# Block 1's first 32 tokens take their expert activations from gathered rows of u: the dense expert layer works on 352 columns

## The chip, the cores and the metric

The kernel runs on one core of a Trainium2 chip. The metric is the device time of one execution in microseconds, the median of several runs. The engines are TensorE (PE), VectorE (DVE), ScalarE (ACT), GpSimd (POOL) and SyncE (SP), which only issues DMAs; ACT and POOL issue DMAs too. Each works through its own queue in order.

## The reference, cut to what matters

One decoder layer on 512 tokens of width 1024, in float32: norm, two kinds of attention, output projection, norm, and then the expert layer below, a last norm. The change is in the expert layer alone. It has 16384 experts of one neuron each; every token chooses 16 of them in each of 8 heads.

```
def chunk(xc):
    q = (xc @ wq).reshape(PEER_CHUNK, PEER_HEADS, 2, PEER_HALF)
    s = jnp.einsum('chpd,hpkd->chpk', q, subkeys)
    s1, i1 = lax.top_k(s[:, :, 0], PEER_TOPK)
    s2, i2 = lax.top_k(s[:, :, 1], PEER_TOPK)
    ...
    eidx = jnp.take_along_axis(cidx, ci, axis=-1)
    g = jax.nn.softmax(cs, axis=-1)
    ug = jnp.take(u_table, eidx, axis=0)
    vg = jnp.take(v_table, eidx, axis=0)
    hid = jnp.einsum('cd,chkd->chk', xc, ug)
    a = jax.nn.gelu(hid, approximate=False) * g
    return jnp.einsum('chk,chkd->cd', a, vg)
```

## The kernel before, in words

Tokens lie in four blocks of 128. Block 0 gets its experts by index: for each of 128 choices a row of u, later a row of v, is gathered for all 128 tokens by an indirect DMA that POOL issues (`gathers`, L488); DVE multiplies a row of u with the tokens and sums (L505), and adds a row of v with its weight to `acc` (L512). The gathered rows go through `rowp`, a pool of four buffers.

Blocks 1 to 3 (384 tokens, `DT`) go through all 16384 experts densely. The experts are cut in 64 items of 256 (`NPAIR`), each of two halves of 128 (c). An item has a hidden part and an output part. Hidden: the item of u is loaded (`wraw`) and split into a high and a low half, whi by ACT (L123) and wlo by DVE (L124); for each half of the item `mm3` (L152) makes 24 matmuls of 128 x 384 into `pj`, and ACT takes the gelu (`hidden`, L526). Output: the gelu is multiplied by the token's gates (DVE, L783), split into ah (ACT) and al (DVE), and multiplied with the item of v, which is loaded and split into vh and vl in the same way: 36 matmuls of 128 x 512 into six accumulators `oa` (L806).

The gates of a token for all 16384 experts are a table, built in the spill stage: `pairs` (L604) chooses experts and gates for a block, `table` (L686) makes one-hot matrices o1, o2 and og (o1 times the gate, as two halves in f16) for eight tokens on DVE, PE multiplies them (L722), ACT copies the result into `gs` (L712), and SP writes it to `Gd` in DRAM, one write for 32 tokens (`GT`).

While that goes on, PE computes the hidden part of the first 28 items (`SPILL`) and writes their gelus to `Hd` in DRAM (`spill`, L535). The dense stage (`dense`, L768) then does the output part of all 64 items, and the hidden part of the other 36 between them; for the 28 it reads `Hd` back (ga). Stored and fresh items alternate by two. The gathers of block 0 run beside the dense stage.

The order: `merge` (L60) interleaves these streams by weights, and the framework then schedules each engine's instructions, and the buffers of the pools, by priorities; what it made is fixed for each engine. In the dense stage DVE's order is that of the code.

Of the kernel before, what the change touches and what calls it, by code (L numbers as in the profile page):

```python
# [10 lines left out]
F32 = mybir.dt.float32  # L11
# [20 lines left out]
NKEY = 128  # L32
DT = T - P
EPS = 1e-6
NEG = -1e30
# [5 lines left out]
NB = 8  # L41
GT = 32
NG = DT // GT
# [28 lines left out]
def tile_kernel(ctx: ExitStack, tc: tile.TileContext, x, w_in, w_f, b_f, w_out, wq, skT, u, v, uT, g1, g2, g2r, gfr,  # L72
# [9 lines left out]
    hres = gdram.tile([T, D], F32, name="hres")  # L82
    Hd = [gdram.tile([P, 2, DT], F32, name=f"Hd{n}") for n in range(SPILL)]

# [147 lines left out]
    with ExitStack() as st:  # L232
# [222 lines left out]
        for c in range(D // WC):  # L455
# [4 lines left out]
            for b in range(0, TB, 2):  # L460
# [62 lines left out]
    def hidden(uu, c, out_):  # L523
        ps = pj.tile([P, T], F32, name="pj")
        mm3(ps[:, :DT], [(uu[0][:, c, k, :], uu[1][:, c, k, :]) for k in range(KC)], XD)
        nc.scalar.activation(out_, ps[:, :DT], AF.Gelu)  # L526

    with ExitStack() as st:
        hsp = pool("hsp", bufs=HB, stack=st)
        rq = pool("rq", stack=st)  # L530
        vv = [rq.tile([P, 2 * NHEAD, TOPK], F32, name=f"vv{b}") for b in range(TB)]
        ii = [rq.tile([P, 2 * NHEAD, TOPK], U32, name=f"ii{b}") for b in range(TB)]
        rp = pool("rp", bufs=2, stack=st)

        def spill(fd, n0, n1):  # L535
            for n in range(n0, n1):
                uu = fd.get()
                hs = hsp.tile([P, 2, DT], F32, name="hs")
# [58 lines left out]
        with ExitStack() as s2:  # L597
# [6 lines left out]
            def pairs(b):  # L604
# [60 lines left out]
                if b == 0:  # L665
                    nc.vector.scalar_tensor_tensor(eidx, res[:, 0, :], float(NKEY), res[:, 1, :], op0=ALU.mult, op1=ALU.add)
                    return
                pt = ptr.tile([P, 3, P], F32, name="ptr")
                for n, src in enumerate((res[:, 0, :], res[:, 1, :], gg.rearrange("p h k -> p (h k)"))):
# [8 lines left out]
                nc.scalar.activation(tg2[:, 0], trg[:, :, None].to_broadcast([P, P, 2]), AF.Copy)  # L678
                nc.vector.tensor_tensor(tg2[:, 1], trg[:, :, None].to_broadcast([P, P, 2]), tg2[:, 0], ALU.subtract)
                yield 2.0  # L680
                for t0 in range(0, P, NB):
                    yield from table(b, t0, tri, tg2)

            tab, work = {}, []

            def table(b, t0, tri, tg2):  # L686
                ts_ = slice(t0, t0 + NB)
                pair = [P, NB, NKEY // 2, 2]

                def pairs_of(t):  # L690
# [3 lines left out]
                o2 = ohp.tile([P, NB, NKEY], F16, name="o2")  # L694
                nc.vector.tensor_tensor(pairs_of(o2), ib, tri[:, 1, ts_, None, :].to_broadcast(pair), ALU.is_equal)
                o1 = ohp.tile([P, NB, NKEY], F16, name="o1")
                nc.vector.tensor_tensor(pairs_of(o1), ib, tri[:, 0, ts_, None, :].to_broadcast(pair), ALU.is_equal)
                og = ohp.tile([P, 2, NB, NKEY], F16, name="og")
                for n in range(2):
                    nc.vector.tensor_tensor(pairs_of(og[:, n]), pairs_of(o1), tg2[:, n, ts_, None, :].to_broadcast(pair), ALU.mult)  # L700
                work.append([b, t0, o2, og, None])
                yield from advance()

            def advance():
                if len(work) > 2 or (work and work[0][4]):
                    b, t0, _, _, pgs = work.pop(0)
                    g = (b - 1) * (P // GT) + t0 // GT
                    if t0 % GT == 0:
                        tab[g] = gsp.tile([P, NKEY, GT], F32, name="gs")
                    for n, pg in enumerate(pgs):  # L710
                        q0 = t0 % GT + 4 * n
                        nc.scalar.activation(tab[g][:, :, q0:q0 + 4].rearrange("p i t -> p t i"), pg, AF.Copy, scale=1.0 / GS)  # L712
                    if t0 % GT == GT - NB:
                        nc.sync.dma_start(Gd[g], tab.pop(g).rearrange("p i t -> p (i t)"))
                for w in work[:-1] if len(work) > 1 else work:
                    if w[4] is None:
                        w[4] = []
                        for t4 in range(0, NB, 4):
                            pg = pgt.tile([P, 4, NKEY], F32, name="pg")
                            for tt in range(4):  # L720
                                for n in range(2):
                                    nc.tensor.matmul(pg[:, tt, :], w[2][:, t4 + tt, :], w[3][:, n, t4 + tt, :], start=(n == 0), stop=(n == 1))  # L722
                            w[4].append(pg)
                yield 2.8

            def gates3():
                for b in range(1, TB):
                    yield from pairs(b)
                while work:
                    yield from advance()  # L730

            L2 = 12.8 + 4.0 + 1.5 + 7.4
            merge((pairs(0), L2), (spill(feed, 0, D0_SPILL), 2.0 * D0_SPILL))
            ga = gathers()
            n1 = SPILL - D0_SPILL
            merge((gates3(), RF * 3 * (L2 + 1.0 + 2.8 * P // NB)), (spill(feed, D0_SPILL, SPILL), 2.0 * n1), (take(ga, D_GATHER), float(D_GATHER)))

    with ExitStack() as st:
# [9 lines left out]
        def load_v(i):  # L748
            if i < NPAIR:
# [3 lines left out]
                if i % 2 == 0:  # L753
# [4 lines left out]
                    gts[i + 1] = gt[:, :, 2:4, :]  # L758
                gas[i] = ep.tile([P, 2, DT], F32, name="ga")
                if n < SPILL:  # L760
# [159 lines left out]
```

## Time and profile before

Median of three runs: 1548.09 us (1547.84 to 1548.88). The profiled execution took 1545.79 us, of which the trace spans 1543.7.

| engine | busy us | share of the span |
|---|---|---|
| PE | 1503.6 | 97% |
| DVE | 1204.2 | 78% |
| ACT | 652.0 | 42% |
| POOL | 371.3 | 24% |

By time: attention and norms up to about 309 us, the query stage to about 403, the spill stage to 704, the dense stage to 1526, the last norm to the end. Busy time is a share over stages with different limits, so it has to be read stage by stage. Matmuls overlap, so what one costs is read from the distance between starts or from a run of them on the chain, not from its length; on DVE, too, an instruction's length overlaps the next by some 0.08 us.

### The profile page before, as it was taken

How to read it: one execution, taken by the hardware profiler on the slowest of the kernel's cores; microseconds unless marked ns; L12 is line 12 of the kernel's file. 1: busy time of each engine (PE TensorE's matmuls, PEld its weight loads, DVE VectorE, ACT ScalarE, POOL GpSimd, SP SyncE). 2: the span in 40 equal slices, each digit the busy share in tenths (PEclk: the TensorE clock that was granted, in tenths of full speed). 3: DMA queues.
4: the chain of work that ended last, by engine and by line, in shares of the span. 5: the costliest groups of instructions: out<-in, count | busy, mean ns of one | idle time of the engine just before them, and what ended most of it. 6: DMA issues, size and time to landing. Idle time of an engine off the chain costs nothing.

```text
span 1543.7 us, 22288 instructions
## 1 busy us (share of the span) xinstructions
PE 1503.6 (97%) x8689; PEld 1339.1 (87%) x8689; DVE 1204.2 (78%) x2250; ACT 652.0 (42%) x809; POOL 371.3 (24%) x273
## 2 busy tenths in 40 slices
PE   7999999999998999999999999999999999999997
PEld 6787888988898898998888899888989888989886
DVE  7555466559999999795788877778787888777886
ACT  6355454422234858485323333333333333333332
POOL 2000000000001000001344444444443443444441
PEclk9999999999999999999999999999999999999999
DMA  6211113322155757569999989999999999999984
GB/s 198 83 55 56 55 55 124 115 101 86 66 185 184 303 214 280 207 262 336 382 338 362 334 328 341 325 349 342 315 351 335 329 360 326 333 329 342 328 284 158
DMA packets 139353, 380.26 MB, mean 246 GB/s; under 512 B 9392, under 2 KB 58800, under 8 KB 134512
## 3 DMA queue, kind: packets, MB, share of 16 engines
q1 hardware_dynamic: 96400, 230.44, 42.1%
q0 software_dynamic: 37664, 134.96, 23.7%
q10 hardware_dynamic: 5184, 13.45, 2.4%
q8 instruction: 68, 1.11, 0.3%
q14 instruction: 37, 0.30, 0.1%
HBM read 338.90 MB, written 40.37 MB: 246 GB/s over the span
## 4 chain that ended last, share of the span: by engine, by line
PE 81%; DVE 12%; ACT 3%; DMA 2%; issue 1%; SPq 0%; ACTq 0%; DVEq 0%
PE pj L152 40%; PE oa L806 33%; DVE wlo L124 3%; PE o L427 2%; PE pg L722 2%; PE s L377 1%; PE t L404 1%; DVE og L700 1%; ACT gs L712 1%; PE xt L140 1%; ACT whi L123 1%; PE psc L587 1%; DMA gt<-Gd 1%; DMA Gd<-gs 1%; DVE eq L659 0%
## 5 line engine op out<-in xcount | busy, mean ns | idle before, releaser
L152 PE MATMUL pj<-xh,whi 128*128 128x384 f32 (+2 forms) x1304 | 454.8, 349 | 5.2 <-ACT hs L526 2.9
L152 PE MATMUL pj<-xh,wlo 128*128 128x384 f32 (+2 forms) x1304 | 453.0, 347 | 1.5 <-DVE wlo L124 1.5
L152 PE MATMUL pj<-xl,whi 128*128 128x384 f32 (+2 forms) x1304 | 452.0, 347 | 0.0
L496 POOL DMA_INDIRECT row<-in_u_dram,eidx x128 | 183.9, 1437 | 706.4 <-DVE hid L505 441.2
L123 ACT ACTIVATE whi<-wraw 128x2048 fp32r<-128x2048 f32 (+1 forms) x89 | 169.7, 1906 | 252.3 <-PE pj L152 244.3
L152 PEld LDWEIGHTS pj<-xh,whi 128*128 128x128 f32 x1304 | 245.8, 188 | 18.5 <-issue 4.7
L152 PEld LDWEIGHTS pj<-xh,wlo 128*128 128x128 f32 x1304 | 246.0, 189 | 11.9 <-DVE wlo L124 2.1
L152 PEld LDWEIGHTS pj<-xl,whi 128*128 128x128 f32 x1304 | 246.0, 189 | 10.2
L124 DVE TENSOR_TENSOR wlo<-wraw,whi 128x2048 fp32r<-128x2048 f32 (+1 forms) x89 | 202.5, 2275 | 61.9 <-ACT whi L123 61.9
L806 PE MATMUL oa<-vh,ah 128*128 128x512 f32 x768 | 238.5, 391 | 2.2 <-ACT ah L123 2.2
L806 PE MATMUL oa<-vh,al 128*128 128x512 f32 x768 | 238.1, 390 | 0.3 <-DVE al L124 0.3
L806 PE MATMUL oa<-vl,ah 128*128 128x512 f32 x768 | 238.0, 390 | 0.0
L496 POOL DMA_INDIRECT row<-in_v_dram,eidx x128 | 177.9, 1390 | 227.0 <-DVE acc L512 196.5
L123 ACT ACTIVATE vh<-vr 128x2048 fp32r<-128x2048 f32 x64 | 122.8, 1919 | 226.9 <-PE oa L806 175.8
L512 DVE SCALAR_TENSOR_TENSOR acc<-row,a,acc 128x1024 f32<-128x1024 f32 x128 | 164.2, 1283 | 23.4 <-DMA row<-in_v_dram,eidx 20.6
L505 DVE CUSTOM_DVE_ANT_0 row<-row,xn 128x1024 f32<-128x1024 f32 x128 | 152.5, 1221 | 29.8 <-DMA row<-in_u_dram,eidx 29.6
L806 PEld LDWEIGHTS oa<-vh,al 128*128 128x128 f32 x768 | 144.5, 188 | 31.4 <-DVE al L124 0.7
L806 PEld LDWEIGHTS oa<-vl,ah 128*128 128x128 f32 x768 | 144.4, 188 | 30.5
L806 PEld LDWEIGHTS oa<-vh,ah 128*128 128x128 f32 x768 | 144.0, 188 | 30.3 <-ACT ah L123 2.5
L124 DVE TENSOR_TENSOR vl<-vr,vh 128x2048 fp32r<-128x2048 f32 x64 | 146.3, 2285 | 0.0
L124 DVE TENSOR_TENSOR al<-ga,ah 128x768 fp32r<-128x768 f32 x64 | 61.3, 958 | 64.4 <-ACT ah L123 64.4
L712 ACT ACTIVATE gs<-pg 128x512 f32<-128x512 f32 x96 | 97.4, 1153 | 18.5 <-PE pg L722 18.1
(207 smaller groups left out, 1588.8 us busy)
## 6 DMA issues: line engine op xcount, KB each, us to landing
wraw<-in_uT_dram SPq DMA_DIRECT2D x64, 1024.0 KB, 6.5
vr<-in_v_dram SPq DMA_DIRECT2D x64, 1024.0 KB, 7.1
Gd<-gs SPq DMA_DIRECT2D x12, 2048.0 KB, 6.7
gt<-Gd SPq DMA_DIRECT2D x32, 768.0 KB, 9.3
wraw<-in_w_in_dram SPq DMA_DIRECT2D x12, 1024.0 KB, 4.8
Hd<-hs ACTq DMA_DIRECT2D x28, 384.0 KB, 3.6
ga<-Hd SPq DMA_DIRECT2D x28, 384.0 KB, 9.0
wraw<-in_wq_dram SPq DMA_DIRECT2D x8, 1024.0 KB, 4.8
```

Source lines behind the costliest of these rows:

```text
L123: nc.scalar.activation(hi, src, AF.Copy)
L124: nc.vector.tensor_sub(lo, src, hi.bitcast(F32))
L140: nc.tensor.matmul(pt[:, kc % 2, e, :], src[:, e, kc * P:(kc + 1) * P], diag[:, e, :], start=True, stop=True)
L152: nc.tensor.matmul(ps, a, c, start=(i == 0), stop=(i == 3 * n - 1))
L377: nc.tensor.matmul(s[:, :n], qs[:, part, h, i * P:n], kT[:, h, :n], start=(part == 0), stop=(part == 1 and g >= 2))
L427: nc.tensor.matmul(o[e * HD:(e + 1) * HD, pr, :], vs[:, j, h * HD:(h + 1) * HD], pts[e][:, j * P:(j + 1) * P], start=(j == 0), stop=(j == i))
L496: nc.gpsimd.indirect_dma_start(out=rows[n], out_offset=None, in_=tab, in_offset=bass.IndirectOffsetOnAxis(ap=eidx[:, k:k + 1], axis=0))
L505: nc.vector.tensor_tensor_reduce(out=t, in0=t, in1=xn0, scale=1.0, scalar=0.0, op0=ALU.mult, op1=ALU.add, accum_out=hid0[:, k:k + 1])
L512: nc.vector.scalar_tensor_tensor(acc, t, a0[:, k:k + 1], acc, op0=ALU.mult, op1=ALU.add)
L712: nc.scalar.activation(tab[g][:, :, q0:q0 + 4].rearrange("p i t -> p t i"), pg, AF.Copy, scale=1.0 / GS)
L722: nc.tensor.matmul(pg[:, tt, :], w[2][:, t4 + tt, :], w[3][:, n, t4 + tt, :], start=(n == 0), stop=(n == 1))
L806: nc.tensor.matmul(oacc[b][d], w[:, c, sl], m[:, c, d * 512:(d + 1) * 512], start=s0, stop=s1)
```

## The change

The first 32 tokens of block 1 leave the hidden part of the dense layer, which works on `DH` = 352 columns. Their activations come from u rows: 32 gathers, in each of which the 128 partitions hold 32 tokens times four groups of choices (`gatherq`), a dot product for each on DVE against `xnq`, the 32 tokens' normed x four times over (written to DRAM as `xqd` and read back), then gelu and gate. Their table therefore holds gate times gelu, in three bf16 parts instead of two f16 ones, and is built last (`tableq`). In the dense stage the other eleven groups are multiplied in place in `gt`, and `gt` is what is split. `SPILL` is 34 instead of 28, `HB` (buffers for hs) 3 instead of 4, and block 1's choice comes before the tables, merged with four items of its own.

```
-SPILL = 28
+SPILL = 34
 D0_SPILL = 4
+D1_SPILL = 4
-HB = 4
+HB = 3
...
-    XD = [(xh[:, k, P:], xl[:, k, P:]) for k in range(KC)]
+    XD = [(xh[:, k, P + GT:], xl[:, k, P + GT:]) for k in range(KC)]
...
+                        for d in range(2):
+                            sd = slice(d * 512, (d + 1) * 512)
+                            xq = hp.tile([GT, 512], F32, name="xq")
+                            nc.vector.scalar_tensor_tensor(xq, hb[0:GT, 1, sd], rs[0:GT, 1:2], g2b[0:GT, sd], op0=ALU.mult, op1=ALU.mult)
+                            nc.scalar.dma_start(xqd[:, sd], xq)
...
+        for s_ in range(NS):
+            nc.scalar.dma_start(xnq[s_ * GT:(s_ + 1) * GT, :], xqd)
...
+            def gatherq():
...
+                        nc.gpsimd.indirect_dma_start(out=rows[k], out_offset=None, in_=u,
+                                                     in_offset=bass.IndirectOffsetOnAxis(ap=eq4[:, k:k + 1], axis=0))
+                for k in range(3):
+                    issue(k)
+                for k in range(HK // NS):
+                    issue(k + 3)
+                    t = rows.pop(k)
+                    nc.vector.tensor_tensor_reduce(out=t, in0=t, in1=xnq, scale=1.0, scalar=0.0, op0=ALU.mult,
+                                                   op1=ALU.add, accum_out=hq4[:, k:k + 1])
+                    yield 1.0
+
+            def tableq():
+                nq = HK // NS
+                for s_ in range(NS):
+                    nc.vector.tensor_copy(aq[0:GT, s_ * nq:(s_ + 1) * nq], hq4[s_ * GT:(s_ + 1) * GT, :])
+                nc.scalar.activation(aq[0:GT], aq[0:GT], AF.Gelu)
+                nc.vector.tensor_mul(aq[0:GT], aq[0:GT], gq)
...
+                for t0 in range(0, GT, NB):
+                    yield from table(t0, t0, trq, tq3, BF16, 1.0)
...
-                for n in range(2):
-                    nc.vector.tensor_tensor(pairs_of(og[:, n]), pairs_of(o1), tg2[:, n, ts_, None, :].to_broadcast(pair), ALU.mult)
+                og = [og[:, 0], og[:, 1]] + ([lp.tile([P, NB, NKEY], dtype, name="og3")] if nparts > 2 else [])
+                for n in range(nparts):
+                    nc.vector.tensor_tensor(pairs_of(og[n]), pairs_of(o1), tg[:, n, ts_, None, :].to_broadcast(pair), ALU.mult)
...
             merge((pairs(0), L2), (spill(feed, 0, D0_SPILL), 2.0 * D0_SPILL))
+            n1 = D0_SPILL + D1_SPILL
+            merge((pairs(1), L2 + 2.0), (spill(feed, D0_SPILL, n1), 2.0 * D1_SPILL))
             ga = gathers()
-            n1 = SPILL - D0_SPILL
-            merge((gates3(), RF * 3 * (L2 + 1.0 + 2.8 * P // NB)), (spill(feed, D0_SPILL, SPILL), 2.0 * n1), (take(ga, D_GATHER), float(D_GATHER)))
+            merge((gates3(), RF * (2 * L2 + 7.0 + 3 * 2.8 * P // NB)), (spill(feed, n1, SPILL), 2.0 * (SPILL - n1)), (gatherq(), 1.2 * HK / NS),
+                  (take(ga, D_GATHER), float(D_GATHER)))
...
-                        a = ga_[:, c, :].rearrange("p (g t) -> p g t", t=GT)
-                        nc.vector.tensor_mul(a, gt[:, :, c, :], a)
+                        a = gt[:, 1:, c, :]
+                        nc.vector.tensor_mul(a, a, ga_[:, c, :].rearrange("p (g t) -> p g t", t=GT))
...
-                    split(ah, al, ga_)
+                    split(*[t.rearrange("p c (g t) -> p c g t", t=GT) for t in (ah, al)], gt.rearrange("p g c t -> p c g t"))
```

Three places show what this does to the order. POOL's queue, from its first gather on, in the kernel before (row_n is a buffer's use, eidx the indices of block 0):

```order
L496 DMA row_4557<-in_u_dram,eidx_99 128x1024
L496 DMA row_4559<-in_u_dram,eidx_99 128x1024
L496 DMA row_4561<-in_u_dram,eidx_99 128x1024
L496 DMA row_4563<-in_u_dram,eidx_99 128x1024
L496 DMA row_6014<-in_u_dram,eidx_99 128x1024
L496 DMA row_7644<-in_u_dram,eidx_99 128x1024
```

And in the changed kernel, where eq4 holds the indices of block 1's 32 tokens:

```order
L723 DMA row_4937<-in_u_dram,eq4_3190 128x1024
L723 DMA row_4939<-in_u_dram,eq4_3190 128x1024
L723 DMA row_4941<-in_u_dram,eq4_3190 128x1024
L723 DMA row_4943<-in_u_dram,eq4_3190 128x1024
L504 DMA row_4946<-in_u_dram,eidx_106 128x1024
L504 DMA row_4948<-in_u_dram,eidx_106 128x1024
L504 DMA row_4950<-in_u_dram,eidx_106 128x1024
L504 DMA row_4952<-in_u_dram,eidx_106 128x1024
L723 DMA row_5009<-in_u_dram,eq4_3190 128x1024
L723 DMA row_5100<-in_u_dram,eq4_3190 128x1024
```

The 32 gathers of block 1 stand in POOL's queue around the first five of block 0, all through the same four buffers.

DVE's queue in the spill stage, at the choice of the last block, in the kernel before (eq and sel2 belong to the choice, wlo to an item of u, o1, o2 and og to a table):

```order
L659 TENSOR_TENSOR eq_6750<-eq_6750,iib_6711 128x2048
L662 TENSOR_TENSOR eq_6750<-eq_6750 128x256x8
L124 TENSOR_TENSOR wlo_6668<-wraw_6444,whi_6667 128x2048
L662 TENSOR_TENSOR eq_6750<-eq_6750 128x256x4
L662 TENSOR_TENSOR eq_6750<-eq_6750 128x256x2
L663 TENSOR_TENSOR sel2_6719<-eq_6750 128x256
L124 TENSOR_TENSOR wlo_6754<-wraw_6575,whi_6753 128x2048
L124 TENSOR_TENSOR wlo_6859<-wraw_6671,whi_6858 128x2048
L695 TENSOR_TENSOR o2_6829<-iota_111,tri_6822 128x1024
```

The same place in the changed kernel:

```order
L678 TENSOR_TENSOR eq_6902<-eq_6902,iib_6826 128x2048 x2
L127 TENSOR_TENSOR wlo_7074<-wraw_6869,whi_7073 128x2048
L681 TENSOR_TENSOR eq_6902<-eq_6902 128x256x8
L731 ISA row_6766,hq4_3191<-row_6766,xnq_3189 128x1024
L731 ISA hq4_3191 128x1
L681 TENSOR_TENSOR eq_6902<-eq_6902 128x256x4
L127 TENSOR_TENSOR wlo_7222<-wraw_6947,whi_7221 128x2048
L681 TENSOR_TENSOR eq_6902<-eq_6902 128x256x2
L682 TENSOR_TENSOR sel2_6863<-eq_6902 128x256
L731 ISA row_6854,hq4_3191<-row_6854,xnq_3189 128x1024
L731 ISA hq4_3191 128x1
L768 TENSOR_TENSOR o2_6987<-iota_118,tri_6980 128x1024
```

Dot products of gathered rows (ISA, with the read of the sum behind each) now stand between the same instructions.

DVE's queue at the end of the spill stage, in the kernel before, from the last og on:

```order
L700 TENSOR_TENSOR og_7520<-o1_7518,tg2_6824 128x1024
L124 TENSOR_TENSOR wlo_7613<-wraw_7317,whi_7612 128x2048
L505 ISA row_4561,hid0_3159<-row_4561,xn0_98 128x1024
L505 ISA hid0_3159 128x1
L505 ISA row_4563,hid0_3159<-row_4563,xn0_98 128x1024
```

In the changed kernel:

```order
L774 TENSOR_TENSOR og_8018<-o1_8016,tq3_7808 128x1024 x2
L774 TENSOR_TENSOR og3_8019<-o1_8016,tq3_7808 128x1024
L127 TENSOR_TENSOR wlo_8155<-wraw_7922,whi_8154 128x2048
L513 ISA row_4950,hid0_3172<-row_4950,xn0_105 128x1024
L513 ISA hid0_3172 128x1
L513 ISA row_4952,hid0_3172<-row_4952,xn0_105 128x1024
```

In both kernels rows of block 0 that were issued early are read only here. In the changed one they keep their buffers while the 32 gathers go through.

## Rows read from the trace of the kernel before

**Rows 1.** Stages: us, busy us (count) of PE PEld DVE ACT POOL, clock, DMA, GB/s
```profile
405.00:704.00 299.00, 287.93 (x2127) 272.12 (x2127) 282.28 (x702) 184.96 (x201) 9.79 (x6) 0.99 0.61 224
...
725.00:1500.00 775.00, 774.73 (x3773) 687.23 (x3773) 624.41 (x655) 263.25 (x231) 340.53 (x242) 1.00 0.94 337
```

**Rows 2.** Chain of waits in order of time: start us, length us, what
```profile
258.96 31.41 PE pj L152 x260
...
703.84 9.08 DMA Gd<-gs
...
800.75 8.34 PE pj L152 x48
809.10 8.20 PE oa L806 x36
```

**Rows 3.** DVE's groups, 725 to 1500 us: busy, mean ns | idle, releaser
```profile
L512 DVE SCALAR_TENSOR_TENSOR acc<-row,a,acc 128x1024 f32<-128x1024 f32 x121 | 155.2, 1283 | 21.9 <-DMA row<-in_v_dram,eidx 19.3 <-DVE acc L512 0.3
L505 DVE CUSTOM_DVE_ANT_0 row<-row,xn 128x1024 f32<-128x1024 f32 x123 | 146.5, 1221 | 29.0 <-DMA row<-in_u_dram,eidx 28.9
L124 DVE TENSOR_TENSOR vl<-vr,vh 128x2048 fp32r<-128x2048 f32 x62 | 141.7, 2285 | 0.0
L124 DVE TENSOR_TENSOR wlo<-wraw,whi 128x2048 fp32r<-128x2048 f32 x34 | 77.8, 2288 | 0.0
L783 DVE TENSOR_TENSOR ga<-gt,ga 128x384 f32<-128x384 f32 x122 | 64.1, 553 | 31.5 <-ACT ga L526 31.5
L124 DVE TENSOR_TENSOR al<-ga,ah 128x768 fp32r<-128x768 f32 x62 | 59.4, 958 | 62.6 <-ACT ah L123 62.6
...
L510 DVE TENSOR_TENSOR a<-a,g 128x16 f32<-128x16 f32 x8 | 1.4, 180 | 6.5 <-ACT a L509 6.5
```

**Rows 4.** PE in order, table matmuls: start us, length us
```profile
502.98 0.96 PE L722 MATMUL pg<-og,o 128*128 128x128 f16 x14
```

**Rows 5.** DVE in order, spill stage: start us, length us [idle <-releaser]
```profile
464.35 1.23 DVE L505 CUSTOM_DVE_ANT_0 row<-row,xn 128x1024 f32<-128x1024 f32 x1 [0.75 <-DMA row<-in_u_dram,eidx]
...
465.50 2.29 DVE L124 TENSOR_TENSOR wlo<-wraw,whi 128x2048 fp32r<-128x2048 f32 x1
467.71 0.08 DVE L550 MATCH_VALUE_LOAD ci<-cs,cw 128x8 f32 x1
...
546.33 2.29 DVE L124 TENSOR_TENSOR wlo<-wraw,whi 128x2048 fp32r<-128x2048 f32 x1
...
707.28 2.29 DVE L124 TENSOR_TENSOR wlo<-wraw,whi 128x2048 fp32r<-128x2048 f32 x1 [7.92 <-ACT whi L123]
```

**Rows 6.** DVE's groups, 405 to 706 us: two kinds
```profile
L700 DVE TENSOR_TENSOR og<-o,tg 128x1024 f16<-128x1024 f16 x96 | 61.9, 683 | 0.0
...
L662 DVE TENSOR_TENSOR eq<-eq 128x512 bf16<-128x512 bf16 x4 | 2.8, 690 | 0.0
```

**Rows 7.** Tile row, 440 to 704 us: issue to landing
```profile
DMA to landing us min/median/max: 4.3/7.3/10.7
```

**Rows 8.** POOL in order of time, gathers of the spill stage
```profile
460.01 1.01 POOL L496 DMA_INDIRECT row<-in_u_dram,eidx  x1 [242.77 <-DVE cw L548]
...
465.86 2.74 POOL L496 DMA_INDIRECT row<-in_u_dram,eidx  x1 [1.07 <-DVE hid L505]
...
546.68 3.18 POOL L496 DMA_INDIRECT row<-in_u_dram,eidx  x1 [78.08 <-DVE hid L505]
```

**Rows 9.** Tile row, 725 to 1105 us: issue to landing
```profile
DMA to landing us min/median/max: 4.4/7.8/11.0
```

**Rows 10.** DVE in order of time, second norm
```profile
300.25 0.69 DVE L465 TENSOR_TENSOR h2b<-h2b,pj 128x512 f32<-128x512 f32 x1 [1.76 <-PE pj L152]
...
302.60 0.16 DVE L472 TENSOR_REDUCE n2ss<-sq 128x2 f32<-128x8 f32 x1 [1.19 <-ACT junk L466]
```

**Rows 11.** ACT in order of time, second norm
```profile
305.25 0.92 ACT L142 ACTIVATE xh<-xt,g2t 128x256 fp32r<-128x256 f32 x2 [2.05 <-PE xt L140]
```

**Rows 12.** Tile hs, all its writes: issue to landing
```profile
DMA to landing us min/median/max: 2.3/3.6/9.2
```

More of the change, by code (lines that the diff above doesn't have):

```diff
@@ L33 @@
 DT = T - P
+GT = 32
+DH = DT - GT
 EPS = 1e-6
@@ L82, in tile_kernel @@
     hres = gdram.tile([T, D], F32, name="hres")
-    Hd = [gdram.tile([P, 2, DT], F32, name=f"Hd{n}") for n in range(SPILL)]
+    xqd = gdram.tile([GT, D], F32, name="xqd")
+    Hd = [gdram.tile([P, 2, DH], F32, name=f"Hd{n}") for n in range(SPILL)]
     cpool = pool("cpool")
@@ L524, in hidden @@
         ps = pj.tile([P, T], F32, name="pj")
-        mm3(ps[:, :DT], [(uu[0][:, c, k, :], uu[1][:, c, k, :]) for k in range(KC)], XD)
-        nc.scalar.activation(out_, ps[:, :DT], AF.Gelu)
+        mm3(ps[:, :DH], [(uu[0][:, c, k, :], uu[1][:, c, k, :]) for k in range(KC)], XD)
+        nc.scalar.activation(out_, ps[:, :DH], AF.Gelu)
     with ExitStack() as st:
@@ L532, in tile_kernel @@
         ii = [rq.tile([P, 2 * NHEAD, TOPK], U32, name=f"ii{b}") for b in range(TB)]
+        NS = P // GT
+        xnq = rq.tile([P, D], F32, name="xnq")
+        eq4 = rq.tile([P, HK // NS], I32, name="eq4")
+        hq4 = rq.tile([P, HK // NS], F32, name="hq4")
+        gq = rq.tile([GT, HK], F32, name="gq")
+        aq = rq.tile([P, HK], F32, name="aq")
+        trq = rq.tile([P, 2, GT, 2], F16, name="trq")
+        nc.gpsimd.memset(aq, 0.0)
+        for s_ in range(NS):
+            nc.scalar.dma_start(xnq[s_ * GT:(s_ + 1) * GT, :], xqd)
         rp = pool("rp", bufs=2, stack=st)
@@ L537, in spill @@
                 uu = fd.get()
-                hs = hsp.tile([P, 2, DT], F32, name="hs")
+                hs = hsp.tile([P, 2, DH], F32, name="hs")
                 for c in range(2):
@@ L679, in pairs, with tables @@
                 nc.vector.tensor_tensor(tg2[:, 1], trg[:, :, None].to_broadcast([P, P, 2]), tg2[:, 0], ALU.subtract)
+                if b == 1:
+                    nc.vector.tensor_copy(trq, tri[:, :, 0:GT, :])
+                parts[b] = tri, tg2
                 yield 2.0
-                for t0 in range(0, P, NB):
-                    yield from table(b, t0, tri, tg2)
+            parts = {}
+            def tables(b):
+                for t0 in range(GT if b == 1 else 0, P, NB):
+                    yield from table((b - 1) * P + t0, t0, *parts[b], F16, 1.0 / GS)
@@ new lines, in gatherq, with issue @@
+            def gatherq():
+                rows = {}
+                def issue(k):
+                    if k < HK // NS:
+                        rows[k] = rowp.tile([P, D], F32, name="row")
+                        nc.gpsimd.indirect_dma_start(out=rows[k], out_offset=None, in_=u,
[8 more added lines that the diff above has]
+                    yield 1.0
@@ new lines, in tableq @@
+            def tableq():
+                nq = HK // NS
+                for s_ in range(NS):
+                    nc.vector.tensor_copy(aq[0:GT, s_ * nq:(s_ + 1) * nq], hq4[s_ * GT:(s_ + 1) * GT, :])
+                nc.scalar.activation(aq[0:GT], aq[0:GT], AF.Gelu)
+                nc.vector.tensor_mul(aq[0:GT], aq[0:GT], gq)
+                pt = ptr.tile([P, 3, P], F32, name="ptr")
+                nc.tensor.transpose(pt[:, 0, :], aq, ident)
+                tra = lp.tile([P, GT], F32, name="tra")
+                tq3 = lp.tile([P, 3, GT, 2], BF16, name="tq3")
+                nc.scalar.activation(tra, pt[:, 0, 0:GT], AF.Copy)
+                twice = [P, GT, 2]
+                nc.vector.tensor_copy(tq3[:, 0], tra[:, :, None].to_broadcast(twice))
+                for n in range(2):
+                    nc.vector.tensor_sub(tra, tra, tq3[:, n, :, 0])
+                    nc.vector.tensor_copy(tq3[:, n + 1], tra[:, :, None].to_broadcast(twice))
+                yield 3.0
+                for t0 in range(0, GT, NB):
+                    yield from table(t0, t0, trq, tq3, BF16, 1.0)
@@ L684, in tile_kernel, with table @@
             tab, work = {}, []
-            def table(b, t0, tri, tg2):
+            def table(tok, t0, tri, tg, dtype, scale):
                 ts_ = slice(t0, t0 + NB)
                 pair = [P, NB, NKEY // 2, 2]
+                nparts = tg.shape[1]
                 def pairs_of(t):
@@ L720, in advance @@
                             for tt in range(4):
-                                for n in range(2):
-                                    nc.tensor.matmul(pg[:, tt, :], w[2][:, t4 + tt, :], w[3][:, n, t4 + tt, :], start=(n == 0), stop=(n == 1))
+                                for n in range(w[5]):
+                                    nc.tensor.matmul(pg[:, tt, :], w[2][:, t4 + tt, :], w[3][n][:, t4 + tt, :], start=(n == 0), stop=(n == w[5] - 1))
                             w[4].append(pg)
@@ L726, in gates3 @@
             def gates3():
-                for b in range(1, TB):
+                yield from tables(1)
+                for b in range(2, TB):
                     yield from pairs(b)
+                    yield from tables(b)
+                yield from tableq()
                 while work:
@@ L758, in load_v @@
                     gts[i + 1] = gt[:, :, 2:4, :]
-                gas[i] = ep.tile([P, 2, DT], F32, name="ga")
+                gas[i] = ep.tile([P, 2, DH], F32, name="ga")
                 if n < SPILL:
```

25 lines of the change are left out of this document (14 added, 11 removed).

## The prediction

> **What bounds the kernel now.** Read first the busy time by stage [rows 1]. TensorE (PE) keeps its full clock of 2.4 GHz in both long stages. In the spill stage (405 to 704 us) VectorE (DVE) is busy 282.3 of 299.0 us, in the dense stage (725 to 1500) PE 774.7 of 775.0. Then the chain of waits [rows 2]: through the dense stage it is PE, item after item, 48 hidden matmuls in 8.34 us and 36 output matmuls in 8.20. Only at the joint it leaves PE, for the last table's write and its read back from 704 us on; that stays as it is. Last, DVE's groups in the dense stage with the idle time ahead of them [rows 3]: 62.6 us for ScalarE's ah (62 times 1.0, written into the order: multiply, ah on ACT, al on DVE), 48.2 for gathered rows (28.9 + 19.3), 6.5 for a gelu, and only 31.5 for PE's hidden layer. With 624.4 busy this is 773.2 of 775: apart from those 31.5 us DVE has no time to spare. TensorE is the bound, and VectorE stands 4% behind it.
>
> **Hidden matmuls, 384 to 352 columns.** One of 384 columns costs 8.34/48 = 173.8 ns, one of 512 columns 8.20/36 = 227.8, one of 256 columns 31.41/260 = 120.8 [rows 2]. That is a line of 0.418 ns a column; 352 columns cost 160.5, an item of 48 costs 7.71 us, 0.63 less. Over 64 items PE has 40.5 us less to do. Where PE is the bound this is gain; in the spill stage it is not.
>
> **SPILL 28 to 34.** Six items move their hidden half from the dense to the spill stage. Dense hidden work goes from 36 x 8.34 = 300.2 to 30 x 7.71 = 231.3: 69 us less. In the spill stage it goes from 233.5 to 262.1; with 800 table matmuls at 69 ns (0.96 us for 14 [rows 4]) and some 6 us of transposes PE needs 323 us there, which stays under what DVE will need.
>
> **Spill stage, on DVE.** Nothing is removed: the 32 tokens still get their table. Added, in distances from one start to the next [rows 5]: six splits wlo at 2.21 = 13.3; 32 dot products at 1.15 = 36.8; the third og part, 4 at 0.68 [rows 6] = 2.7; some 16 small ones (index, gate and hq4 copies, the three parts), nearest row 0.18 each with its overlap [rows 3], taken as 2. Sum 54.8 us, on the engine that already fills the stage.
>
> **The wait that comes with the 32 gathers.** POOL's order shows it: of its first eight gathers four belong to block 0 (row_4946 to row_4952), but DVE reads row_4948 only in the middle of the stage, row_4950 and row_4952 after the last table. They hold buffers, four in all, so most gathers of block 1 find one free buffer: the next is issued only when the last has been read. Behind a late row DVE stands still in order, and with it wlo, the tables and PE. What a lone gather takes to land no row shows directly; six in this stage took 4.3 at least and 7.3 in the middle [rows 7], five of them close together. Counting out of DVE's order what stands between one dot product and the next that needs its buffer (from row_6766 to row_6854 one wlo of 2.21 and three operations of at most 0.69 [rows 6], so some 4 us), the shortfalls add up to 2 us if a gather lands in 4.3 (six of 34 come late), to 11 in 5.5 (eight), to 33 in 7.3 (eighteen). I take 11: the first gather, alone, took 4.3, and POOL's issue is often longer than its 1.01. It took 2.74 and 3.18 where it started 0.4 us into a wlo [rows 8], and ended about 1 us behind that wlo's end [rows 5]; DVE runs such operations through the whole stage. The Trainium skill (SBUF — State Buffer, Who interferes with whom) says that a tensor_tensor takes only the read interface it shares with GpSimd, and infers that this doesn't hold up descriptor generation. These two issues disagree with it, and the measurement decides. By the page every gather would come at its shortest, and the spill stage would be 9 us shorter than below.
>
> Of the stage's 16.7 us of DVE idle time 4.7 belong to the wait for whi at its end [rows 5]; they stay. Of the other 12, paced by PE and ACT, 6 go, since PE will have 36 us to spare. Spill stage: 54.8 + 11 - 6 = 60 us longer. Bounds: 54.8 + 2 - 12 = 45 and 54.8 + 33 = 88.
>
> **Dense stage.** PE alone would make it 69 us shorter. But count DVE from 725 to 1500, which holds 62 items and 34 splits of u [rows 3]. Six splits fewer: 13.3. The multiply on 352 for 384 columns saves at most 553 x 32/384 = 46 ns, 122 times: 5.6, taken as 4. What remains is 624.4 - 17.3 + 62.6 + 6.5 + 48.2 = 724 us, all of it DVE's own or waits that don't come from PE; PE needs 774.7 - (34 x 8.34 - 28 x 7.71) = 707. So DVE takes over: 51 us shorter if row waits stay at 48. They won't. 244 gathers in 736 instead of 775 us come every 3.02 instead of 3.18; a buffer's round, from the read that frees it to the read that needs it, shrinks from 4 x 3.18 - 1.15 = 11.6 to 10.9 us, and the slowest landing is 11.0, the median 7.8 [rows 9]. Transfers get tighter too: 337 GB/s at a busy share of 0.94 [rows 1] is 358 at a full one, and 261 - 5 = 256 MB then need 714 of 736 us. Row waits lie between 48 (51 us gained) and twice that (3 gained); I take 60, nearest to today's: 736, so 40 us shorter.
>
> **Norm.** The two xq multiplies on DVE fall where it waits today, 1.76 and 1.19 us [rows 10]: nothing, or 0.6 each. ScalarE's queue matters more: the first xnq load waits until both xqd writes have landed, and the xh copies behind it are on the path; the first starts at 305.25, when PE has transposed [rows 11]. The second xqd goes out near 302.3; the nearest write, of Hd, takes 2.3 at least and 3.6 in the middle [rows 12]. So xh starts 0 to 1.5 us later, plus issue time: 0 to 3, taken as 1.5.
>
> **Sum.** The profiled execution took 1545.8 (span 1543.7 and 2.1 around it), 2.3 under the median of three runs. 1545.8 + 1.5 + 60 - 40 = 1567.3; on the median's scale 1570 us, 1.4% slower.
>
> **Rivals.** (a) PE keeps the dense stage: the row waits are only DVE being early, and vanish as it gets late. For it: PE never waited for DVE in the 775 us, and 31.5 us of waiting for PE show that DVE was ahead at times. Against: 117 of the 149 us of DVE's waits have other causes. The dense stage then gains 69, and with 45 to 60 in the spill stage the time is 1526 to 1541 on the median's scale: faster. It decides if row waits fall under 31 us. (b) The two cancel: dense 55 to 62 shorter, spill as taken, within a few us of 1548. (c) The one free buffer is dear: with landings of 7.3 the spill stage is 88 longer, and the dense stage 30 shorter: 1548.1 + 1.5 + 88 - 30 = 1608. For it: the median landing; a DMA share of 0.61 in that stage already [rows 1], and 16.8 MB on top. Against: a lone gather shares with little. It decides from landings above 6.5 us.
>
> **Chances.** Forecast (1555 to 1592) 0.55; (a) 0.22; (b) 0.10; (c) 0.13. A change of 0.2%, here 3 us, is about what a measurement of this kernel can tell from none. Faster 0.24: (a) and a little of (b). Same 0.08, most of (b). Slower 0.68. Range 1535 to 1603: it leaves out the lower part of (a) and most of (c). The forecast's own range is 1555 to 1592.
>
> **What would show it.** Right: DVE's busy time in the spill stage up by 50 to 58 us and the last table copy at about 765; waits of DVE for rows of u there, at the close pairs of dot products, 5 to 20 us in sum. In the dense stage PE no longer full (some 95%), DVE's waits for ga near zero, for rows 55 us or more, and PE waiting for al or vl; 48 hidden matmuls in 7.7 us. Wrong: PE still at 99% or more in the dense stage, with its length near 750 us; or the last copy before 750 us; or matmuls of 352 columns as long as those of 384, which would leave the dense stage only the six moved items, 50 us.

## The result, and the profile after

The changed kernel takes 1593.38 us (median of four runs, 1587.28 to 1598.70), the kernel before 1547.96 beside it: a ratio of 1.0298 (95% interval 1.0250 to 1.0346). It is 45 us slower, where 22 were forecast. The profiled execution took 1597.15 us, one of the longer of the four, with a span of 1595.4, 51.7 longer than before; the stages below are read from it, so they add up to 51 and not to 45:

| stage | forecast | measured | read from |
|---|---|---|---|
| norm | +1.5 | +0.3 | first queries' copy 312.92 to 313.17 us |
| spill stage | +60 | +76.1 | last table's write issued at 703.8 and 779.9 |
| dense stage | -40 | -25.0 | first to last output matmul, 809.5 and 784.6 us long |

The stages of the kernel after answer to [rows 1], with the same columns (stretch and length; busy time and count of PE, PEld, DVE, ACT and POOL; granted clock; DMA share; GB/s):

```profile
405.00:780.00 375.00, 334.43 (x2460) 315.38 (x2460) 337.17 (x790) 200.55 (x221) 59.79 (x38) 0.96 0.68 245
...
801.00:1576.00 775.00, 745.66 (x3608) 641.02 (x3607) 621.87 (x664) 245.88 (x218) 343.95 (x247) 0.98 0.93 336
```

In the spill stage DVE's work grew from 282.3 to 337.2 us, by 54.9, and its idle time from 16.7 to 37.8 (up to 780). In the dense stage PE is no longer full: 745.7 of 775, where it had 774.7. DVE's waits in the spill stage (who waited for whom: us in total, times, longest):

```profile
DVE row L731 <- DMA row<-in_u_dram,eq: 25.1, 12, 6.1
DVE wlo L127 <- ACT whi L126: 5.2, 3, 3.1
DVE row L513 <- DMA row<-in_u_dram,eidx: 2.0, 1, 2.0
DVE o L768 <- PE pg L796: 1.5, 2, 1.3
```

27.1 of its idle us are gathered rows that had not landed; the other idle time fell from 16.7 to 10.7. DVE's groups in the dense stage, 801 to 1576 us, answer to [rows 3]:

```profile
L520 DVE SCALAR_TENSOR_TENSOR acc<-row,a,acc 128x1024 f32<-128x1024 f32 x128 | 164.2, 1283 | 33.5 <-DMA row<-in_v_dram,eidx 31.2
L513 DVE CUSTOM_DVE_ANT_0 row<-row,xn 128x1024 f32<-128x1024 f32 x123 | 146.5, 1220 | 47.8 <-DMA row<-in_u_dram,eidx 47.5
...
L127 DVE TENSOR_TENSOR al<-gt,ah 128x768 fp32r<-128x768 f32 x64 | 61.3, 958 | 66.6 <-ACT ah L126 66.6
L863 DVE TENSOR_TENSOR gt<-gt,ga 128x352 f32<-128x352 f32 x126 | 60.3, 519 | 3.1 <-ACT ga L534 3.1
```

Waits for rows rose from 48.2 to 78.7 us, and the wait for the gelu of PE's hidden layer fell from 31.5 to 3.1. DVE is late, and PE waits for what comes behind DVE (its waits from 801 to 1576 us):

```profile
PE oa L886 <- ACT ah L126: 25.4, 12, 5.2
PE oa L886 <- DVE al L127: 3.9, 15, 0.3
```

The columns do what was counted: in PE's order the 48 hidden matmuls of an item start at 1224.46, the output matmuls behind them at 1232.07, 7.61 us [rows 2: 8.34].

```profile
1224.46 0.33 PE L155 MATMUL pj<-xh,whi 128*128 128x352 f32 x1
...
1232.07 0.63 PE L886 MATMUL oa<-vh,ah 128*128 128x512 f32 x2
```

How one late row reaches PE, and what it costs: first DVE in order of time (start us, length us, idle time before it and what ended it), then ACT, PE, and the stretches.

```profile
877.96 1.23 DVE L513 CUSTOM_DVE_ANT_0 row<-row,xn 128x1024 f32<-128x1024 f32 x1 [4.01 <-DMA row<-in_u_dram,eidx]
...
879.11 0.95 DVE L863 TENSOR_TENSOR gt<-gt,ga 128x352 f32<-128x352 f32 x2
```

```profile
880.10 0.84 ACT L126 ACTIVATE ah<-gt 128x768 fp32r<-128x768 f32 x1 [10.20 <-DVE gt L863]
```

```profile
875.32 0.61 PE L886 MATMUL oa<-vl,ah 128*128 128x512 f32 x2
881.00 1.22 PE L886 MATMUL oa<-vh,ah 128*128 128x512 f32 x2 [5.06 <-ACT ah L126]
```

```profile
875.00:880.00 5.00, 0.93 (x5) 0.43 (x3) 2.04 (x4) 0.00 (x0) 2.41 (x3) 1.00 1.02 407
880.00:885.00 5.00, 4.00 (x9) 2.94 (x10) 4.09 (x4) 2.64 (x2) 0.45 (x1) 0.53 0.95 321
885.00:890.00 5.00, 5.00 (x19) 3.98 (x19) 3.67 (x10) 1.06 (x2) 3.84 (x3) 0.79 0.96 318
890.00:895.00 5.00, 5.00 (x24) 4.15 (x23) 5.00 (x5) 1.92 (x1) 0.55 (x2) 1.00 0.88 333
```

The row came 4.0 us late; the multiply behind it in DVE's queue, ACT's ah and PE's next output matmul followed. PE stood 5.06 us. When it went on, its clock was granted at 0.53, near the lower of its two levels (1.2 of 2.4 GHz): a pair of matmuls took 1.22 us for 0.61. It was back at 1.00 from 890 on. Whether the slow clock made the stage longer is not shown: DVE, which sets the pace here, waited for PE only 3.1 us in 775.

### The profile page after: what moved, and what is told of

Its sections match the earlier page's. It is cut to its first block, busy times and chain, and to the rows that moved or that the text cites. A ratio compares the mean times of both kernels' runs of the same rounds, so it can differ in the third digit from the quotient of the medians.

```text
span 1595.4 us, 22534 instructions
## 1 busy us (share of the span) xinstructions
PE 1494.6 (94%) x8722; PEld 1312.5 (82%) x8722; DVE 1241.5 (78%) x2336; ACT 646.3 (41%) x811; POOL 417.0 (26%) x306
## 5 line engine op out<-in xcount | busy, mean ns | idle before, releaser
L155 PE MATMUL pj<-xh,whi 128*128 128x352 f32 (+2 forms) x1304 | 446.8, 343 | 21.4 <-ACT hs L534 15.0
L155 PE MATMUL pj<-xh,wlo 128*128 128x352 f32 (+2 forms) x1304 | 444.4, 341 | 5.1 <-DVE wlo L127 5.1
L155 PE MATMUL pj<-xl,whi 128*128 128x352 f32 (+2 forms) x1304 | 444.7, 341 | 0.0
L155 PEld LDWEIGHTS pj<-xh,whi 128*128 128x128 f32 x1304 | 249.9, 192 | 36.2 <-ACT hs L534 16.9
L886 PE MATMUL oa<-vh,ah 128*128 128x512 f32 x768 | 243.3, 398 | 25.6 <-ACT ah L126 25.4
L155 PEld LDWEIGHTS pj<-xl,whi 128*128 128x128 f32 x1304 | 250.2, 192 | 10.0
L504 POOL DMA_INDIRECT row<-in_u_dram,eidx x128 | 177.1, 1384 | 294.8 <-DVE hid L513 247.6
L886 PE MATMUL oa<-vh,al 128*128 128x512 f32 x768 | 243.2, 397 | 3.9 <-DVE al L127 3.9
L126 ACT ACTIVATE ah<-gt 128x768 fp32r<-128x768 f32 x64 | 54.1, 845 | 271.7 <-DVE gt L863 263.9
L723 POOL DMA_INDIRECT row<-in_u_dram,eq x32 | 53.3, 1667 | 405.5 <-ACT hs L534 237.4
```

Of the source, the lines that this page charges most:

```text
L126: nc.scalar.activation(hi, src, AF.Copy)
L155: nc.tensor.matmul(ps, a, c, start=(i == 0), stop=(i == 3 * n - 1))
L504: nc.gpsimd.indirect_dma_start(out=rows[n], out_offset=None, in_=tab, in_offset=bass.IndirectOffsetOnAxis(ap=eidx[:, k:k + 1], axis=0))
L723: nc.gpsimd.indirect_dma_start(out=rows[k], out_offset=None, in_=u, in_offset=bass.IndirectOffsetOnAxis(ap=eq4[:, k:k + 1], axis=0))
L886: nc.tensor.matmul(oacc[b][d], w[:, c, sl], m[:, c, d * 512:(d + 1) * 512], start=s0, stop=s1)
```

## Experiments

Each edit is shown against the changed kernel unless it says otherwise. Ratios are to the kernel before, with 95% intervals; "dense stage" means first to last output matmul, "last write" the issue of the last table's write.

**Block 0's gathers behind the 32.**

```
+            def rows_in_turn():
+                yield from gatherq()
+                yield from take(ga, D_GATHER)
-            ... (gatherq(), 1.2 * HK / NS), (take(ga, D_GATHER), float(D_GATHER)))
+            ... (rows_in_turn(), 1.2 * HK / NS))
```

> The gathers of block 0 start only when the 32 of block 1 are done, so these have all four row buffers. Theory 1 (the free buffer: three of four buffers were held by block 0's early rows): VectorE's waits for rows in the spill stage fall from 27 us to 6 or less, the last table is written about 20 us earlier than in the changed kernel (at 758 to 763 instead of 779.9), the time is 1570 to 1577 us. Rival (the gather itself is late: POOL's issue beside VectorE's work, or its landing): the waits for rows stay at 18 us or more and the time within 5 us of 1593.

1570.79 us, 1.0161 (1.0142 to 1.0180); the last write at 756.3. The waits for rows in the spill stage, in the same view as above:

```profile
DVE row L731 <- DMA row<-in_u_dram,eq: 3.0, 2, 2.7
```

22 of the waits' 25 us went, as theory 1 says: with all four buffers free for the 32, few of them arise. The last write came 23.6 us earlier, a little more than expected. The dense stage stayed at 782 us.

**Dot products without gathers.**

```
-                for k in range(3):
-                    issue(k)
+                t = rowp.tile([P, D], F32, name="row")
...
-                    nc.vector.tensor_tensor_reduce(out=t, in0=t, in1=xnq, ...
+                    nc.vector.tensor_tensor_reduce(out=t, in0=xnq, in1=xnq, ...
```

> The 32 dot products are made, but of xnq with itself, so nothing is gathered for them (their tokens' activations are therefore not the right ones). No wait for rows can be left in the spill stage. If those waits (27 us) were all that the gathers cost, the stage ends 20 to 27 us earlier than in the changed kernel and the time is 1566 to 1574; by theory 1 it then agrees with the run that gives the 32 gathers all buffers, within 6 us. If the 16.8 MB of rows also hold up the loads of uT and the writes of Hd and the tables, this run is shorter than that one by more than 6 us.

1554.09 us, 1.0056 (1.0039 to 1.0073): 17 us shorter than the run above, so the sign of the second expectation came true. It doesn't show that the rows hold up other transfers: freed of their indices, 14 of the 32 dot products had moved ahead of the spill stage (the first to 314.6 us), where DVE has room. 14 times 1.22 is 17 us, as much as the whole difference. A later run, with one gather, keeps the dot products in their place.

**Neither gathers nor dot products.**

```
-            ... (gatherq(), 1.2 * HK / NS), (take(ga, D_GATHER), float(D_GATHER)))
+            ... (take(ga, D_GATHER), float(D_GATHER)))
+        nc.gpsimd.memset(hq4, 0.0)
```

> Neither gathers nor dot products (the 32 tokens' activations are left out, their table is built from zeros). Takes away 36.8 us of VectorE's work beside the 27 us of waits. By my count VectorE would need 300 us of its own in the stage from 405, PE 333 us by its busy time of the changed kernel, of which some is slow clock: PE becomes the bound, the stage ends at 735 to 745 instead of 779.9, the time is 1550 to 1560. If VectorE stays the bound all the way, the whole 64 us come back: 1530.

1550.70 us, 1.0019 (1.0003 to 1.0035); the last write at 734.5, a little under the stretch expected. PE is the bound there, with 316.3 us busy of 329, DVE 301.3:

```profile
405.00:734.00 329.00, 316.31 (x2429) 304.12 (x2428) 301.28 (x726) 200.14 (x219) 7.23 (x6) 0.98 0.62 225
```

Of 64 us that went from DVE 45 came back; from there on PE's 34 items are the length of the stage, which is still 31 us longer than before.

**SPILL 28.**

```
-SPILL = 34
+SPILL = 28
```

> The changed kernel with 28 items in the spill stage as before, so six items go back. Theory 2 (in the dense stage VectorE and its waits are the bound, not PE): spill stage 13 to 16 us shorter, dense stage 2 to 19 us longer (PE alone needs 801 - 36 x 0.63 = 778 us with 36 items), time 1580 to 1598. Rival (PE still bounds the dense stage): six items of 7.71 us come on top there, 46 us, time 1620 to 1626.

1591.69 us, 1.0288 (1.0271 to 1.0305). The dense stage took 786 us, 1 more than with 34, and not 46 more. Theory 2 holds, with PE full here (first line) where it had 29 us to spare with 34:

```profile
796.00:1580.00 784.00, 783.30 (x3932) 691.05 (x3931) 642.58 (x693) 268.67 (x250) 344.07 (x247) 1.00 0.94 339
```

```profile
DVE row L731 <- DMA row<-in_u_dram,eq: 34.7, 13, 7.3
```

So the two bounds cross between 28 and 34 items: the move bought nothing. The other number was missed: the spill stage became 3 us shorter (last write at 776.7), not 13 to 16. Six wlo went, and the waits for rows grew from 25.1 to 34.7 us: with less work between them the gathers, one by one through one buffer, set more of the pace; that is a reading, and was not tested apart. PE, waiting more, was granted a clock of 0.89 from 405 to 776, where the changed kernel had 0.96.

**A fifth row buffer in the dense stage**, on top of the first edit.

```
+        more.append(pool("row2", bufs=1, stack=st))
...
-                rows[n] = rowp.tile([P, D], F32, name="row")
+                rows[n] = (rowp if n < 1 or n % 5 else more[0]).tile([P, D], F32, name="row")
...
-            issue(n + 3)
+            while at <= n + (4 if more else 3):
+                issue(at)
+                at += 1
```

> On top of the run with block 0's gathers behind the 32: a fifth row buffer in the dense stage, and gathers issued one step further ahead. There the dense stage (first to last output matmul) took 782 us, in the changed kernel 784.5, before 809.6. Theory 3 (the round of a row buffer is the bound: four buffers at one gather per 3.06 us give 12.2 us less 1.2 for the read, against landings of 7.7 in the middle and 11.0 at most): a fifth gives 3 us more, VectorE's waits for rows in the dense stage fall from 79 us to under 40, the stage takes 745 to 765 us, the time is 1535 to 1553. Rival (the transfers' bandwidth is the bound, busy share 0.94): the landings grow by the same 3 us, the waits stay above 60 and the stage above 775.

1528.24 us, 0.9875 (0.9857 to 0.9894): 42.6 us less than with four, and faster than the kernel before. The dense stage took 741 us. Stage and time are both shorter than the ranges expected, and the signs are those of theory 3. Its stretch, and DVE's two row groups from 776 to 1516:

```profile
776.00:1516.00 740.00, 737.18 (x3644) 645.13 (x3644) 628.24 (x684) 253.88 (x234) 352.30 (x246) 1.00 0.96 352
```

```profile
L525 DVE SCALAR_TENSOR_TENSOR acc<-row,a,acc 128x1024 f32<-128x1024 f32 x128 | 164.2, 1283 | 8.6 <-DMA row<-in_v_dram,eidx 5.7
L518 DVE CUSTOM_DVE_ANT_0 row<-row,xn 128x1024 f32<-128x1024 f32 x123 | 145.4, 1221 | 8.8 <-DMA row<-in_u_dram,eidx 8.7
```

Waits for rows fell from 78.7 to 14.4 us, PE is full and its clock at 1.00. The DMAs moved 352 GB/s here and 336 with four buffers: bandwidth was not the bound with four.

**Rows of half the length.**

```
-D_GATHER = 2
+D_GATHER = 0
...
+        uh, vh_ = [t.rearrange("n (h d) -> (n h) d", h=2) for t in (u, v)]
...
-    nc.gpsimd.indirect_dma_start(out=rows[n], ...
+    nc.gpsimd.indirect_dma_start(out=rows[n][:, :D // 2], ...
```

> Block 0's rows are fetched at half their length, 2 KB for 4, 256 of them all in the dense stage; VectorE still works on 1024 elements, by reading the half twice (block 0's result is therefore not the reference's). 66 of the 261 MB of the dense stage go, with the same number of gathers, buffers and VectorE operations. If the rows come late because the transfers are full (bandwidth, or landings that grow with the load): landings fall below 6 us, waits for rows below 30, the dense stage takes 740 to 755 us. If a gather's time does not hang on bytes: landings stay above 7 and the stage above 775.

1526.33 us, 0.9874 (0.9851 to 0.9897). No gather of block 0 is issued in the spill stage here, so the 32 have all four buffers, and the run to compare with is the one of the first edit, 1570.79. The dense stage took 742 us with four buffers, at a DMA share of 0.80:

```profile
771.00:1513.00 742.00, 738.64 (x3650) 644.74 (x3649) 633.66 (x686) 253.17 (x233) 344.23 (x249) 1.00 0.80 266
```

Waits for rows in the whole stage were 37 us for 77, over the 30 expected (from 850 to 1450 33, where the changed kernel had 69). So the time a row takes under load and the number of buffers are two sides of the same wait; how long these gathers took to land is not in the trace.

**No gathers of block 0 in the dense stage**, on top of the first edit, with four buffers.

```
-            merge((dense(), ...), (ga, GF * (2.0 * HK - D_GATHER)))
+            merge((dense(), ...))
```

> The dense stage without block 0's gathers and their VectorE work (254 of 256 steps left out, so block 0's result is missing). It shows what TensorE alone makes of the stage. By the prediction 69 us less than before, so 740 us, and TensorE never waits: time about 1528. If ScalarE's ah, the splits or the loads of v hold TensorE up without the gathers too, the stage stays above 755.

1519.85 us, 0.9829 (0.9811 to 0.9846). The dense stage is 738 us, with PE full and its clock at 1.00: the floor that PE sets, 72 under before. With five buffers the kernel is within 4 us of it.

```profile
770.00:1506.00 736.00, 736.00 (x3642) 645.25 (x3643) 329.29 (x303) 249.54 (x225) 0.00 (x0) 1.00 0.52 176
```

**One gather for 32 dot products.**

```
-                for k in range(3):
-                    issue(k)
+                issue(0)
+                r0 = rows.pop(0)
+                t = rowp.tile([P, D], F32, name="row")
...
-                    nc.vector.tensor_tensor_reduce(out=t, in0=t, in1=xnq, ...
+                    nc.vector.tensor_tensor_reduce(out=t, in0=r0, in1=xnq, ...
```

> The 32 dot products stand where the changed kernel has them, but all on one gathered row (31 of 32 gathers left out, so the 32 tokens' activations are not the right ones). The run without any gather was 17 us shorter than the one with free buffers, but there 14 of the dot products had been moved to before 460 us, into VectorE's free time, which is 17 us by itself. If that is all: time within 4 us of 1571. If the traffic of the rows (16.8 MB) or POOL's issue costs the stage something beside the waits: 1554 to 1562.

1565.70 us, 1.0128 (1.0108 to 1.0148); the last write at 750.3, 6 us ahead of the run with free buffers. The time falls between the two expectations. Both runs waited 3.0 us for rows (here 0.5 for the one row and 2.5 for one of block 0), and from 405 us to the last write DVE's idle time is nearly the same, 9.6 and 10.4 us. What differs is its work, 335.6 and 340.9 us: there one wlo more and two more dot products of block 0, 4.4 us, stand ahead of the last write. So neither the rows' traffic nor POOL's issue is shown to cost the stage anything beside the waits.

**The kernel before, with the fifth buffer.** The edit of the fifth buffer, made in the kernel before:

```
-                rows[n] = rowp.tile([P, D], F32, name="row")
+                rows[n] = (rowp if n < 1 or n % 5 else more[0]).tile([P, D], F32, name="row")
```

> The kernel before with the fifth row buffer in its dense stage, nothing else. If its dense stage is TensorE's (busy 774.7 of 775 us), the waits for rows that go (48 us) were none of its time: 1547, within 3 us. If those waits held it up too, as in the changed kernel, it gets faster by 10 us or more, and the fifth buffer is a gain by itself and not what the changed kernel lacked.

1544.87 us, 0.9989 (0.9980 to 0.9999). DVE's groups from 725 to 1500 answer to [rows 3]:

```profile
L517 DVE SCALAR_TENSOR_TENSOR acc<-row,a,acc 128x1024 f32<-128x1024 f32 x121 | 155.1, 1282 | 3.9 <-DMA row<-in_v_dram,eidx 1.3
L510 DVE CUSTOM_DVE_ANT_0 row<-row,xn 128x1024 f32<-128x1024 f32 x123 | 144.9, 1218 | 0.1
...
L789 DVE TENSOR_TENSOR ga<-gt,ga 128x384 f32<-128x384 f32 x122 | 65.1, 553 | 79.6 <-ACT ga L531 77.8 <-ACT whi L123 1.7
```

The waits for rows are gone, 48.2 to 1.3, and the wait for PE's gelu took their place, 31.5 to 77.8. The dense stage stayed as long as it was, 809.4 us for 809.5, and the time fell by 1.2 us against the 1546.07 of the kernel before beside it. In the kernel before, a late row cost next to nothing: DVE only waited a little sooner.

**The move of six items alone**: the kernel before with the fifth buffer, and

```
-SPILL = 28
+SPILL = 34
```

> The kernel before with the fifth row buffer and SPILL 34: the move of six items alone, without the 32 gathered tokens and with 384 columns. If what pays in the change is the columns, and the move only carries TensorE's work to where it has room: here the spill stage has 11 us of room for 6 x 8.34 = 50 us, so it gets 40 to 50 us longer and the dense stage 50 shorter, time 1538 to 1550. If the move pays by itself (the spill stage longer only by VectorE's 13 us): 1510 to 1520.

1548.48 us, 1.0019 (1.0009 to 1.0029). The last write came at 753.3, 49.5 later, and the dense stage took 763 us, 47 less. PE's work was carried from one full stage into another. It also shows which engine the spill stage of the kernel before hung on: the 49.5 us are PE's work on six items (50), not DVE's (13), and DVE came to wait for PE by way of ACT, whose whi waits for a buffer that PE has read (DVE from 405 to 754 us; 9.8 in the kernel before):

```profile
DVE wlo L124 <- ACT whi L123: 31.4, 8, 7.9
```

**More items in the spill stage**: block 0's gathers behind the 32, five buffers, and SPILL 36 or 38.

```
-SPILL = 34
+SPILL = 36
```

> The changed kernel with block 0's gathers behind the 32, the fifth row buffer (1528 us) and SPILL 36. By the profile of that kernel TensorE bounds the dense stage again (600 of 600 us busy from 850 to 1450) and VectorE the spill stage (341.0 of 351, TensorE 329.7): two items more cost 4.4 to 15 us there and give 15.4 back, time 1517 to 1528. If VectorE is too near its bound in the dense stage (508.9 busy of 600, and 62 of waits for ah), the dense stage gives less than 8 and the time is 1526 to 1535.

> The same with SPILL 38. TensorE would need 329.7 + 31 = 360 us in the spill stage and so become its bound there: 15 to 28 us longer, against 31 shorter in the dense stage (741 to 710, where VectorE and its waits by my count need 699 to 708): 1512 to 1530. If the dense stage is VectorE's from here on, the waits for rows come back (above 40 us from 850 to 1450) and the time is above the one with SPILL 36.

With 36: 1515.15 us, 0.9791 (0.9774 to 0.9808), 2 us under the range expected and faster than both kernels. The last write came at 752.9, no later than with 34, so PE's idle time took in the two items. The dense stage took 735 us, 7 less; that is under the 8 us that the second reading named, and less than half of the 15.4 that PE saves, so the dense stage is no longer PE's alone. The median is 13 us under the run with 34, the traced execution 9. With 38: 1526.09, 0.9865 (0.9840 to 0.9889); the last write at 766.3 and the dense stage 723, so the spill stage now pays 13 us for 11 that the dense stage gains, and the read back of the last table takes 4 more before the dense stage starts. The waits for rows did not come back (15.5 us from 850 to 1450).

## Why the prediction was wrong

The direction and the work were right: slower, DVE the new bound in the dense stage, PE's need there 69 us less (72 measured without gathers), DVE's added work in the spill stage 54.8 us (54.9). The measured 1593 lies inside the outer range and 1 us above the forecast's own. Two terms of the sum were mis-sized, both downwards, so that nothing cancelled, and both are the same thing, the wait for a gathered row.

**The row stalls in the spill stage: 11 forecast, 27 measured**, and that is the whole miss of this stage: the other two terms, +54.8 and -6, came out as +54.9 and -6. The step named the cause, one free buffer, and counted DVE's work between a read and the next; then it used one landing time, 5.5, for all. The count of DVE's work was good: with the moments at which DVE wanted each row in the changed kernel, 5.5 us for every landing makes 12 us of waits. The middle was well chosen too (5.8 in the kernel with 28 items, whose gathers also wait for buffers that block 0 holds), but landings there run from 4.3 to 11.1, and the stalls are made by the slow ones. In the changed kernel the twelve rows that DVE waited for were read 4.3 to 17.6 us after their issue began; five of them took over 10 us, and these five make 15.2 of the 25.1 us. The longest wait, of 6.1 us, belongs to the gather that POOL issued at 554.20, in 0.94 us; DVE read it at 564.56. Why such rows land late stays open. How much the free buffer matters shows in the same rows: from 574 to 660 us, when one more of block 0's rows had been read and two buffers were free, DVE waited 2.3 us, in the rest of the stage 22.8. One wait in that time came from a gather held up at its issue, and cost 2.1 us (POOL in order of time):

```profile
554.20 0.94 POOL L723 DMA_INDIRECT row<-in_u_dram,eq  x1 [5.22 <-DVE cs L568]
...
589.68 13.84 POOL L723 DMA_INDIRECT row<-in_u_dram,eq  x1 [3.54 <-DVE hq L731]
```

The bound of 33 us held. POOL's long issues, one of the reasons given for 11, made little of it: of the twelve late rows only two had an issue over 1.2 us (3.24 and 13.84), with 4.6 us of waits. Given the rows of before, 4.3 to 10.7 us, the value should have been taken from a spread of landings, not from one.

**The row waits in the dense stage: 60 taken, 78.7 measured**, and with them -40 became -25: 19 us of waits, 15 us of time. The step compared the mean round of a buffer, 10.9 us, with landings of 7.8 and at most 11.0 [rows 9], and so saw few late rows. But DVE reads rows in bunches. Worked out from the reads in order of time from 860 to 1460 in the changed kernel, from the read that frees a buffer to the moment DVE wants the next row in it: 10.9 us on average, just as forecast, but under 9.0 in over a quarter of the reads; with five buffers 13.3, and under 9.0 in 6%. It is the short rounds that meet a landing of 7 or 8 us. The kernel before has the bunches too, 11.4 on average and under 9.0 in a fifth of the reads, so they could have been read from its trace.

**Rival (a)**, that row waits are only DVE being early, was right of the kernel before, where taking them away changed the dense stage by 0.1 us, and wrong of the changed one, where DVE had only 3.1 us of waiting for PE left to give. The same waits were slack in one kernel and length in the other. **Rival (c)** named the mechanism of the spill stage with 88 us; 76 lie between it and the forecast's 60.

**Small ones.** The spill stage of the kernel before was read as full of DVE's work; the run with six items alone shows that it was PE's, 288 of 299 us busy. That didn't change the sum, since DVE is the bound there once its 54.8 us are added. The norm cost 0.3 for 1.5: on ACT the xh copy of [rows 11] started at 306.43 for 305.25, behind the load of xnq at 306.08, but the copy of the first queries only 0.25 us later, at 313.17 for 312.92. That POOL's issue takes longer beside DVE's two-operand work is borne out: in the changed kernel the middle is 0.94 us for the 73 gathers issued while DVE was idle, and 1.90 for the 31 issued during a wlo. That this makes 9 us of the stage is not borne out, as the late rows show. The Trainium skill (SBUF — State Buffer, Who interferes with whom) infers that a tensor_tensor does not hold it up. The issue of 13.84 us began at 589.68 and ended at 603.5, while DVE ran wlo and f16 tensor_tensor operations one behind the other from 591.6: the trace disagrees again. Why this one took so long stays open, since the 23 issued during the tables' f16 operations took at most 1.15.

Where did the gain go? PE needs 72 us less in the dense stage. 52 went into the spill stage, which no buffer gives back (756.3 for 703.8): 31 of them stand without gathers and dot products too (734.5), where PE's six more items set the length, and 22 come with the gathers and DVE's dot products. Of the rest, 24 went to the missing row buffers there and 43 to one in the dense stage. With both buffers given, 1528 us; with the items dealt out again, 1515.

## What to carry to other kernels

Where TensorE is full, waits of the engine behind it can be free (48 us of them cost nothing here), and the time that a change takes off TensorE can make them dear at once: before speeding up the bound, look at what the second engine waits for, and give it the buffer first. Size a stream of gathers by its shortest rounds and its slow landings, not by the two means; and look who holds the buffers of a shared pool, since prefetched rows of a stream that wasn't due yet held two or three of the four. Moving work between two stages pays only into idle time: six items from full to full gave nothing, two into PE's idle time gave 9 to 13 us.

## What the runs showed of the hardware that was not expected

- An indirect gather's issue on POOL takes longer beside some work of DVE. In the changed kernel the middle is 0.94 us while DVE was idle (73 gathers), 1.86 beside the adds to `acc` (66) and 1.90 beside a wlo (31). One took 13.84 us, while DVE ran tensor_tensor operations without a gap; these took 0.73 us in that time and 0.68 behind it. In the run with five buffers the longest was 9.41. What made these two so long is not shown.
- A stop of PE of 5.06 us was followed by a granted clock of 0.53 and 0.79 in the next two stretches of 5 us, worked out as some 7 us at the lower level, so it cost PE more than its length. After a second stop, of 5.15 us at 1139, it was 0.59 in the first 5 us.
- A DMA share of 0.93 at 336 GB/s looked full and was not: with one more gather in flight the same engines moved 352, and 368 from 1000 to 1200 us, there at a share of 1.00.
